# The opening of a two-layer encoder with TensorE in written order up to the first scores

## The chip, the cores and the metric

The kernel runs on one core of a Trainium2 chip. The time is that of one execution on the device, in microseconds. The engines are named as in the profile: PE is TensorE (PEld its weight loads), DVE is VectorE, ACT is ScalarE, POOL is GpSimd, and SP issues most DMAs.

## What is computed

The input is a grid of 512 tokens (8 rows of 64) with 1024 features in float32. There are two residual layers, each followed by a squared-ReLU MLP of width 4096, and a last RMSNorm. Only the first layer's mixing matters here:

```python
hn = rmsnorm(h, norm_mix[0])
z = hn @ w_in                                    # 512 + 128 + 128 + 384 + 256 + 32 columns
qa, ka, va, cq, ckv, kr = jnp.split(z, EVEN_SPLITS, axis=-1)
qa = axial_rope(rmsnorm(qa, a_q_norm), row, col)     # 8 heads of 64
ka = axial_rope(rmsnorm(ka, a_k_norm), row, col)     # 2 heads of 64
oa = block_attention(qa, ka, va, HEAD_DIM ** -0.5)
qb = rmsnorm(cq, b_q_norm) @ b_w_uq              # group B: low-rank query and key/value latents
kvb = rmsnorm(ckv, b_kv_norm) @ b_w_ukv
ob = block_attention(q_full, k_full, vb, (B_NOPE + B_ROPE) ** -0.5)
h = h + concat(oa, ob) @ w_out
```

The second layer is a neighbourhood attention over an 8 x 16 window.

## The kernel before

The activations lie transposed, features on partitions and the 512 tokens along the free axis. Where precision matters an operand is split into two fp32r tiles, a high half (a rounded copy, by ACT) and a low half (the difference, by DVE or POOL), and a product is three matmuls (`mm3`, lines 506 to 508): high by high, high by low, low by high.

**The order of work.** The program is written as one stream. A scheduler arranges each engine's instructions by priority (program order) and by its own estimate of when operands are ready. So before the change TensorE's instructions in the opening do not run as written. Where `tc.manual_schedule` names an engine, that engine follows the program; `tc.keep_in_program_order` does so for one instruction.

**The opening.** Row block k of x (128 features) is transposed by `make_x(k)`, scaled by the norm's gain and split into `X[k]` (lines 545 to 551). `load_w(k)` brings 768 columns of that row block of `w_in`; `use_w(k, m)` adds its three products to bank m. The six banks are the key (m = 0), the value (m = 1) and four pairs of query heads (m = 2 to 5). Row blocks 0 to 5 go bank by bank; then, for each bank, row blocks 6 and 7 close it ("the last rows", lines 759 to 770). `sumsq_acc` adds up the squares of x (line 522); `compact_r` sums them over partitions with the ones vector (line 527) and takes the reciprocal root `r0`, the RMSNorm's scale of each token, which is applied late.

**Behind a bank.** `ev_ka` takes the key: squares by ACT and their sum over each head by a plain fp32 matmul (`stat`, lines 595 and 596), the small transposes that bring the sums to tokens on partitions (`stats_to_tok`, line 580), `rsqrt` on DVE (an integer start and three Newton rounds, lines 159 to 169), the scale spread by transposes (line 535), rotary positions (`rope`, lines 565 to 571), and the split key, whose two halves SP copies across partitions (line 670). `ev_va` transposes the value. `ev_q` does the squares of a query pair (lines 595, 596) and copies the query out (line 608). `q_scales` turns the sums of all eight query heads into scales at once, `rope_q(0)` rotates the first pair (lines 565 to 571) and splits it (lines 622 and 623).

**The attention.** `attend` goes through 64 steps, one for each head and block of 128 queries: scores (line 996), then on DVE scale and row minimum (line 1000, needs the head's scale), ACT's exponential (line 1002), a division by POOL (line 1004), transposes and split of the weights (lines 971 to 974) and the product with the value (line 984). `Fill` puts other TensorE work between these steps, 1.5 us of it for each: first the products for `cq` and `ckv` ("z", columns 768 and up), the latents' norms, then group B's projections. `fill.credit` counts what is owed.

**The end.** `last_mlp` does the last RMSNorm for each of four token blocks: `add` (line 1595), squares with a row sum (line 1599), a root on ScalarE (line 1609), a Newton step on DVE, two scalings and the stores. A placeholder root (line 1656) is written ahead of the second column half.

Of the kernel before, what the change touches and what calls it, by code (L numbers as in the profile page):

```python
# [8 lines left out]
F32 = mybir.dt.float32  # L9
# [26 lines left out]
def encoder_kernel(ctx: ExitStack, tc: tile.TileContext, ins, out, dbg=None):  # L36
# [103 lines left out]
    ACT.activation(act0, zeros, AF.Copy)  # L140
# [383 lines left out]
    def compact_r(acc):  # L524
# [5 lines left out]
        return rsqrt(v, 4)  # L530
# [43 lines left out]
    def stats_to_tok(bk, n, name):  # L574
# [11 lines left out]
        y = rsqrt(v, 4 * n)  # L586
# [4 lines left out]
    QA = []  # L591

    def stat(src, idx, total, lhs, bk, n):
        sq = scratch()
        ACT.activation(sq, src, AF.Square)
        PE.matmul(bk[0:n, :], lhs, sq, start=idx == 0, stop=idx == total - 1)

    def ind1(t):
        return cst[:, C_I1 + 10 * t : C_I1 + 10 * t + 10]
# [4 lines left out]
    QS = [Slot(F32) for _ in range(2)]  # L604

    def ev_q(t, b):
        stat(b, t, 4, ind1(t)[:, 0:8], hold["stq"], 8)
        ACT.activation(QS[t // 2].t[:, S * (t % 2) : S * (t % 2) + S], b, AF.Copy, scale=gT[:, 45:46])

# [41 lines left out]
    def ev_ka(b):  # L651
        st = stb()
        stat(b, 0, 1, ind1(4)[:, 8:10], st, 2)
        kg = scratch()
        ACT.activation(kg, b, AF.Copy, scale=gT[:, 46:47])
        rs = stats_to_tok(st, 2, "rsA")
        krot = rope(kg, cosA, sinA, sw16)
        bk = stb()
        rx = scratch()
        DVE.tensor_copy(rx.rearrange("p (i v e) -> p i v e", i=4, v=2),  # L660
                        rs.unsqueeze(3).to_broadcast([P, 4, 2, 64]))
        bcast_cols(lambda i: rx[:, i * P : (i + 1) * P], P, bk)
        kn = scratch()
        DVE.tensor_tensor(kn, krot, bk, op=ALU.mult)
        for v in range(2):
# [4 lines left out]
            SP.dma_start(f32(kt[z : z + 64, :, :]), f32(kt[a : a + 64, :, :]))  # L670

    def ev_va(b):
        vs = scratch()
        ACT.activation(vs, b, AF.Copy)
        tb = stb()
        for i in range(4):
            PE.transpose(tb[:, i * P : (i + 1) * P], vs[:, i * P : (i + 1) * P], ident)
        for i in range(4):
# [3 lines left out]
                                     op0=ALU.mult, op1=ALU.subtract)  # L682

# [22 lines left out]
    def q_scales():  # L706
        rs = stats_to_tok(hold["stq"], 8, "rsQ")
        sc = keep([P, 4, 8], F32, "scA")
        DVE.tensor_scalar(sc, rs, -0.125, 1.0, op0=ALU.mult, op1=ALU.mult)
        hold["scA"] = sc  # L710
# [46 lines left out]
    sumsq_acc(6, acc)  # L757
    sumsq_acc(7, acc)
    for m in range(6):
        for k in (6, 7):  # L760
            use_w(k, m)
        if m == 0:
            DVE.tensor_copy(r0, compact_r(acc))
            DVE.tensor_tensor(r0sq, r0, r0, op=ALU.mult)
            ev_ka(banks[0])
        elif m == 1:
            ev_va(banks[1])
            hold["stq"] = stb()
        else:
            ev_q(m - 2, banks[m])  # L770
    q_scales()
    rope_q(0)
# [33 lines left out]
    def latents():  # L806
# [4 lines left out]
        sB = stats_to_tok(b, 2, "rsB")  # L811
# [211 lines left out]
    def heads_A():  # L1023
        for h in range(8):
# [13 lines left out]
            yield dict(e=e, done=done, scale=lambda i, h=h: hold["scA"][:, i, h : h + 1],  # L1038
# [50 lines left out]
    fill.add("z", product(w_in, 0, XP, tiles(768, 384), ev_cq, three))  # L1089
# [495 lines left out]
    def last_mlp():  # L1585
# [43 lines left out]
        def down(k0, nk, c, up, tail):  # L1629
# [4 lines left out]
            def run():  # L1634
# [12 lines left out]
                for j in range(4):  # L1647
# [94 lines left out]
```

## Time and profile before

| | us |
|---|---|
| median of 3 runs | 1183.11 (1182.50 to 1183.43) |
| the profiled execution | 1181.52 |
| its span, first to last instruction | 1179.7 |
| its granted TensorE clock | 0.998 of full |

Times within the profile count from the span's start. A row of the order of time gives start, duration, engine, line, operation, what is written and read (by tile name, the buffer's number left out), shapes and a count; in brackets stands how long the engine idled before it and whose signal ended that. A row of the busy time by stage gives a stretch, its length, and the busy microseconds (with the number of instructions) of PE, PEld, DVE, ACT and POOL, then the granted clock, the DMA engines' busy share and GB/s. A row of the grouped instructions gives line, engine, operation, tiles, shape, count, then total busy time and the mean in ns. ACT loads function tables four times in this execution: at 1.78 us, at 3.29 (for line 1656, which the scheduler had moved to the start), at 68.53 (for the exponential of line 1002) and at 1164.28 (for line 1609).

### The profile page before, as it was taken

How to read it: one execution, taken by the hardware profiler on the slowest of the kernel's cores; microseconds unless marked ns; L12 is line 12 of the kernel's file. 1: busy time of each engine (PE TensorE's matmuls, PEld its weight loads, DVE VectorE, ACT ScalarE, POOL GpSimd, SP SyncE). 2: the span in 40 equal slices, each digit the busy share in tenths (PEclk: the TensorE clock that was granted, in tenths of full speed). 3: DMA queues.
4: the chain of work that ended last, by engine and by line, in shares of the span. 5: the costliest groups of instructions: out<-in, count | busy, mean ns of one | idle time of the engine just before them, and what ended most of it. 6: DMA issues, size and time to landing. Idle time of an engine off the chain costs nothing. (4 is left out here: it accounts for less than half of the span.)

```text
span 1179.7 us, 20002 instructions
## 1 busy us (share of the span) xinstructions
PE 1161.2 (98%) x7200; PEld 1019.6 (86%) x7200; DVE 891.2 (76%) x1528; ACT 646.4 (55%) x1097; POOL 540.8 (46%) x683
## 2 busy tenths in 40 slices
PE   9999999999999999999999999999999999999997
PEld 8667788887898999989998998988889899998995
DVE  5588998878866488798884676667986677779775
ACT  5477676764444366743453555555553366664344
POOL 3257242215453878429802232231367458825920
PEclk9999999999999999999999999999999999999999
DMA  7223325222435523225226565433243223342322
GB/s 250 69 58 93 83 57 134 72 63 81 145 88 180 192 73 99 90 90 161 72 73 171 131 174 133 128 106 116 89 153 108 81 73 93 90 133 71 126 73 72
DMA packets 111235, 128.04 MB, mean 109 GB/s; under 512 B 9139, under 2 KB 88928, under 8 KB 111136
## 3 DMA queue, kind: packets, MB, share of 16 engines
q1 hardware_dynamic: 108080, 119.30, 33.7%
q0 software_dynamic: 2304, 6.31, 2.3%
q8 instruction: 57, 0.93, 0.3%
q10 hardware_dynamic: 752, 1.15, 0.3%
q14 instruction: 42, 0.34, 0.1%
HBM read 104.32 MB, written 6.29 MB: 94 GB/s over the span
## 5 line engine op out<-in xcount | busy, mean ns | idle before, releaser
L309 DVE TENSOR_TENSOR wlo<-a,whi 128x896 fp32r<-128x896 f32 x133 | 164.3, 1239 | 76.1 <-ACT whi L308 74.0
L308 ACT ACTIVATE whi<-a 128x896 fp32r<-128x896 f32 x133 | 125.8, 949 | 156.0 <-PE o L507 34.7
L506 PE MATMUL mm<-a,whi 128*128 128x512 f32 x473 | 190.3, 405 | 0.6 <-ACT a L832 0.4
L507 PE MATMUL mm<-a,whi 128*128 128x512 f32 x473 | 187.4, 396 | 0.0
L508 PE MATMUL mm<-a,wlo 128*128 128x512 f32 x473 | 187.0, 396 | 0.0
L202 DVE TENSOR_TENSOR wlo<-raw,whi 128x1024 fp32r<-128x1024 f32 (+4 forms) x113 | 131.6, 1168 | 57.0 <-ACT whi L212 56.7
L302 POOL TENSOR_TENSOR a<-a 128x128 f32<-128x128 f32 x133 | 91.8, 690 | 143.0 <-DMA a<-in_ffn_w_up_dram 96.8
L212 ACT ACTIVATE whi<-raw 128x1024 fp32r<-128x1024 f32 (+3 forms) x116 | 112.0, 967 | 77.4 <-PE s L507 19.4
L303 POOL TENSOR_TENSOR a<-a 128x256 f32<-128x256 f32 x133 | 122.9, 924 | 10.4
L304 POOL TENSOR_TENSOR a<-a 128x128 f32<-128x128 f32 x133 | 112.7, 847 | 10.4
L395 PE MATMUL mm<-a,wlo 128*128 128x256 f32 x390 | 109.8, 282 | 0.7 <-DVE wlo L309 0.7
L393 PE MATMUL mm<-a,whi 128*128 128x256 f32 x390 | 109.6, 281 | 0.0
L394 PE MATMUL mm<-a,whi 128*128 128x256 f32 x390 | 109.4, 281 | 0.0
L508 PEld LDWEIGHTS mm<-a,wlo 128*128 128x128 f32 x473 | 88.6, 188 | 21.6 <-issue 1.7
L506 PEld LDWEIGHTS mm<-a,whi 128*128 128x128 f32 x473 | 88.9, 188 | 20.5 <-issue 1.4
L507 PEld LDWEIGHTS mm<-a,whi 128*128 128x128 f32 x473 | 89.0, 188 | 19.4 <-issue 1.7
L1004 POOL TENSOR_SCALAR p<-p,ti 128x512 f32<-128x512 f32 x64 | 46.3, 724 | 88.3 <-DVE ti L1003 74.3
L1438 POOL TENSOR_SCALAR p<-p,ti 128x256 f32<-128x256 f32 x64 | 35.6, 567 | 105.0 <-DVE ti L1437 91.9
L393 PE MATMUL t<-a,whi 128*128 128x256 f32 x280 | 78.7, 281 | 0.0
L394 PE MATMUL t<-a,whi 128*128 128x256 f32 x280 | 78.6, 281 | 0.0
L395 PE MATMUL t<-a,wlo 128*128 128x256 f32 x280 | 78.5, 280 | 0.0
L395 PEld LDWEIGHTS mm<-a,wlo 128*128 128x128 f32 x390 | 73.4, 188 | 1.5 <-DVE wlo L309 1.5
(335 smaller groups left out, 3251.6 us busy)
## 6 DMA issues: line engine op xcount, KB each, us to landing
a<-in_ffn_w_up_dram SPq DMA_DIRECT2D x100, 256.0 KB
raw<-in_ffn_w_down_dram SPq DMA_DIRECT2D x42, 512.0 KB
a<-in_ffn_w_down_dram SPq DMA_DIRECT2D x33, 256.0 KB
raw<-in_od_w_qkv_dram SPq DMA_DIRECT2D x64, 128.0 KB
raw<-in_ffn_w_up_dram SPq DMA_DIRECT2D x12, 512.0 KB
raw<-in_ev_w_in_dram SPq DMA_DIRECT2D x12, 384.0 KB
a<-a SPq DMA_DIRECT2D x18, 256.0 KB
bias<-bx SPq DMA_DIRECT2D x16, 256.0 KB
```

The costliest lines, as they stand in the source:

```text
L202: z = lambda: (eng or DVE).tensor_tensor(to, src, f32(high), op=ALU.subtract)
L212: ACT.activation(hi[:, 0:m], raw[:, 0:m], AF.Copy)
L303: POOL.tensor_tensor(r[:, 4:6], r[:, 2:3].to_broadcast([P, 2, P]), r[:, 0:7:6], op=ALU.add)
L304: POOL.tensor_tensor(r[:, 7], r[:, 3], r[:, 5], op=ALU.subtract)
L308: ACT.activation(hi[:, 0:896], raw[:, 128:1024], AF.Copy)
L309: DVE.tensor_tensor(lo[:, 0:896], raw[:, 128:1024], f32(hi[:, 0:896]), op=ALU.subtract)
L393: PE.matmul(o, wh, x[:, 0], start=kp == 0 and n in (0, 1, 3, 5), stop=False, skip_group_check=True)
L394: PE.matmul(o, wh, x[:, 1], start=False, stop=False, skip_group_check=True)
L395: PE.matmul(o, wl, x[:, 0], start=False, stop=kp == self.np - 1, skip_group_check=True)
L506: PE.matmul(o, wh, xh, start=first, stop=False)
L507: PE.matmul(o, wh, xl, start=False, stop=False)
L508: PE.matmul(o, wl, xh, start=False, stop=last)
```

## The change

- **TensorE in written order.** From the last rows up to the scales of the last six query heads, TensorE follows the program. `ev_ka` and `ev_va` become generators whose parts are placed between banks by hand. The first z product is made here, and thirteen of its steps (three matmuls each) are placed between the parts; the rest goes to the fill, which starts with a credit of -6.
- **Split squares.** `squares` splits ACT's squares into a high half (DVE copy) and a low half (POOL subtraction) in a slot of its own; `stat` multiplies each half by an fp32r copy of the indicator columns, `ind`.
- **Roots on ScalarE.** `rsqrt_root` takes ACT's Sqrt, DVE's reciprocal and one Newton step. `r0`, the key's scale and the first two heads' scales use it. The first ACT operation is a Sqrt, and an Exp placeholder follows the last root of the opening.
- **The first two heads' scales on their own.** `q_scales` is called for heads 0 and 1 alone, and later for the other six, which keep the Newton start.
- The last two sums of x's squares go from POOL to DVE. The placeholder root of the last stage reads `ss[:, 3:4]`, a result of that stage, in place of a constant.

```diff
-    ACT.activation(act0, zeros, AF.Copy)
+    ACT.activation(act0, zeros, AF.Sqrt)
...
+    def rsqrt_root(v, n):
+
+        root, hv, y, a, y2 = (tiny(n) for _ in range(5))
+        ACT.activation(root, v, AF.Sqrt)
+        DVE.tensor_scalar(hv, v, -0.5, 1.0, op0=ALU.mult, op1=ALU.mult)
+        DVE.reciprocal(y, root)
+        DVE.tensor_tensor(a, y, y, op=ALU.mult)
+        DVE.tensor_tensor(a, a, hv, op=ALU.mult)
+        DVE.scalar_tensor_tensor(y2, a, 1.5, y, op0=ALU.add, op1=ALU.mult)
+        return y2
...
-    def stat(src, idx, total, lhs, bk, n):
-        sq = scratch()
+    ind = keep([P, 50], F32R, "ind")
+    DVE.tensor_copy(ind, cst[:, C_I1 : C_I1 + 50])
+
+    def squares(src):
+
+        sq, t = scratch(), Slot()
         ACT.activation(sq, src, AF.Square)
-        PE.matmul(bk[0:n, :], lhs, sq, start=idx == 0, stop=idx == total - 1)
+        hi, lo = t.pair()[:, 0, :], t.pair()[:, 1, :]
+        DVE.tensor_copy(hi, sq)
+        POOL.tensor_tensor(lo, sq, f32(hi), op=ALU.subtract)
+        return t
+
+    def stat(t, idx, total, lhs, bk, n):
+        for z in range(2):
+            PE.matmul(bk[0:n, :], lhs, t.pair()[:, z, :], start=idx == 0 and z == 0, stop=idx == total - 1 and z == 1)
+        t.free()
...
     def ev_ka(b):
-        st = stb()
-        stat(b, 0, 1, ind1(4)[:, 8:10], st, 2)
+
+        sq = squares(b)
         kg = scratch()
         ACT.activation(kg, b, AF.Copy, scale=gT[:, 46:47])
+        krot = rope(kg, cosA, sinA, sw16)
+        yield
+        st = stb()
+        stat(sq, 0, 1, ind1(4)[:, 8:10], st, 2)
+        yield
         rs = stats_to_tok(st, 2, "rsA")
-        krot = rope(kg, cosA, sinA, sw16)
-        bk = stb()
         rx = scratch()
...
+        yield
+        bk = stb()
         bcast_cols(lambda i: rx[:, i * P : (i + 1) * P], P, bk)
...
-    sumsq_acc(6, acc)
-    sumsq_acc(7, acc)
-    for m in range(6):
+    sumsq_acc(6, acc, DVE)
+    sumsq_acc(7, acc, DVE)
+
+    first_z = product(w_in, 0, XP, tiles(768, 384), ev_cq, three)
+
+    def more(n):
+        for _ in range(n):
+            next(first_z)
+
+    def last_rows(m):
         for k in (6, 7):
             use_w(k, m)
...
+    with tc.manual_schedule(engines={mybir.EngineType.PE}):
+        last_rows(0)
+        ka = ev_ka(banks[0])
+        next(ka)
+        last_rows(1)
+        va = ev_va(banks[1])
+        next(va)
+        DVE.tensor_copy(r0, compact_r(acc, rsqrt_root))
+        DVE.tensor_tensor(r0sq, r0, r0, op=ALU.mult)
+        last_rows(2)
+        ev_q(0, banks[2])
+        next(ka)
+        last_rows(3)
+        next(ka)
+        ev_q(1, banks[3])
+        last_rows(4)
+        rope_q(0)
+        next(va)
+        ev_q(2, banks[4])
+        last_rows(5)
+        next(ka)
+        ev_q(3, banks[5])
+        st0 = stb()
+        stat(hold["sq0"], 0, 1, ind1(0)[:, 0:2], st0, 2)
+        more(3)
+        q_scales(st0, 0, 2)
+
+        tc.keep_in_program_order(ACT.activation(tiny(1), zeros, AF.Exp))
+        more(1)
+        stq = stb()
+        for t in (1, 2, 3):
+            stat(hold[f"sq{t}"], t - 1, 3, ind1(t)[:, 2:8], stq, 6)
+            more(3)
+        q_scales(stq, 2, 6, rsqrt)
...
-    fill.add("z", product(w_in, 0, XP, tiles(768, 384), ev_cq, three))
+    fill.add("z", first_z)
+    fill.credit = -6.0
...
-                        ACT.activation(tiny(1), ones[:, 0:1], AF.Sqrt)
+                        ACT.activation(tiny(1), ss[:, 3:4], AF.Sqrt)
```

More of the change, by code (lines that the diff above doesn't have):

```diff
@@ L522, in sumsq_acc, with compact_r @@
             (eng or POOL).tensor_tensor(acc, acc, sq, op=ALU.add)
-    def compact_r(acc):
+    def compact_r(acc, root=rsqrt):
         b = stb()
@@ L529, in compact_r @@
         DVE.tensor_scalar(v, b[:, 0:4], 1.0 / D, EPS, op0=ALU.mult, op1=ALU.add)
-        return rsqrt(v, 4)
+        return root(v, 4)
     def bcast_cols(col_ap, nparts, bk):
@@ L572, in rope, with stats_to_tok @@
         return c
-    def stats_to_tok(bk, n, name):
+    def stats_to_tok(bk, n, name, root=rsqrt_root):
         st = scratch()
@@ L604, in encoder_kernel @@
     QS = [Slot(F32) for _ in range(2)]
+    scA = {}
     def ev_q(t, b):
-        stat(b, t, 4, ind1(t)[:, 0:8], hold["stq"], 8)
+        hold[f"sq{t}"] = squares(b)
         ACT.activation(QS[t // 2].t[:, S * (t % 2) : S * (t % 2) + S], b, AF.Copy, scale=gT[:, 45:46])
@@ L674, in ev_va @@
         ACT.activation(vs, b, AF.Copy)
+        yield
         tb = stb()
@@ L704, in stat2, with q_scales @@
             POOL.tensor_tensor(sq[:, 0:512], sq[:, 0:512], sq[:, 512:1024], op=ALU.add)
-    def q_scales():
-        rs = stats_to_tok(hold["stq"], 8, "rsQ")
-        sc = keep([P, 4, 8], F32, "scA")
+    def q_scales(bk, h0, n, root=rsqrt_root):
+        rs = stats_to_tok(bk, n, f"rsQ{h0}", root)
+        sc = keep([P, 4, n], F32, f"scA{h0}")
         DVE.tensor_scalar(sc, rs, -0.125, 1.0, op0=ALU.mult, op1=ALU.mult)
-        hold["scA"] = sc
+        for h in range(n):
+            scA[h0 + h] = [sc[:, i, h : h + 1] for i in range(4)]
     mt0 = [512, 640, 0, 128, 256, 384]
@@ L1036, in done @@
                         KA[t // 2].free()
-            yield dict(e=e, done=done, scale=lambda i, h=h: hold["scA"][:, i, h : h + 1],
+            yield dict(e=e, done=done, scale=lambda i, h=h: scA[h][i],
                        passes=lambda i, q=q, k=k, e=e: [(q[:, e, i * P : (i + 1) * P], k[:, z, :]) for z in range(2)],
```

19 lines of the change are left out of this document (5 added, 14 removed).

## The prediction

> **What bounds the kernel now.** I read the page's first line, then the busy time by stage, then the order of time around the stage that the change rewrites.
>
> ```profile
> span 1179.7 us, 20002 instructions
> ```
>
> ```profile
> 48.00:60.00 12.00, 11.97 (x45) 5.89 (x43) 7.14 (x20) 8.18 (x17) 2.57 (x2) 1.00 0.38 99
> 60.00:72.00 12.00, 11.13 (x47) 8.10 (x48) 9.63 (x30) 6.46 (x12) 3.83 (x3) 1.00 0.28 82
> 72.00:84.00 12.00, 10.89 (x67) 8.39 (x65) 9.96 (x29) 10.46 (x24) 6.78 (x10) 1.00 0.20 46
> 84.00:100.00 16.00, 14.58 (x85) 11.95 (x85) 14.37 (x34) 12.66 (x29) 10.77 (x12) 1.00 0.33 91
> ...
> 230.00:1179.00 949.00, 938.38 (x5999) 842.78 (x5997) 710.86 (x1105) 493.50 (x790) 449.93 (x574) 1.00 0.37 110
> ```
>
> The columns are the stretch, its length, then the busy microseconds of PE, PEld, DVE, ACT and POOL, the granted clock and the DMA share. TensorE is busy for 938 of the last 949 us, at full clock (1.00). The change rewrites the opening, and what follows is a queue of TensorE work: a microsecond won or lost on TensorE before about 100 us is carried to the end unless a later wait swallows it. Busy is not full speed, so I price TensorE by the steps from one start to the next:
>
> ```profile
> 57.01 0.40 PE L506 MATMUL mm<-a,whi 128*128 128x512 f32 x1
> ...
> 57.34 1.02 PE L596 MATMUL t<-sc,cst 128*8 128x512 f32 x2
> ...
> 58.29 0.50 PE L507 MATMUL mm<-a,whi 128*128 128x512 f32 x1
> ...
> 58.63 0.40 PE L508 MATMUL mm<-a,wlo 128*128 128x512 f32 x1
> ...
> 60.25 0.39 PE L507 MATMUL mm<-a,whi 128*128 128x512 f32 x1
> ...
> 60.48 0.40 PE L508 MATMUL mm<-a,wlo 128*128 128x512 f32 x1
> ...
> 61.03 0.41 PE L580 MATMUL t<-cst,sc 8*128 8x8 f32 x4
> ...
> 61.37 0.51 PE L507 MATMUL mm<-a,whi 128*128 128x512 f32 x1
> ...
> 65.92 0.50 PE L996 MATMUL s<-a,a 128*128 128x512 f32 x1 [0.55 <-DVE a L623]
> ```
>
> Two dense products start 0.23 apart (60.25, 60.48). One sum of squares (L596, plain fp32) holds TensorE from 57.34 to 58.29, 0.95, and the products on either side of it step by 0.33 and 0.34 instead of 0.23: 1.15 in all. The first scores start at 65.92.
>
> **The change part by part.** *Split squares on TensorE.* Each of the five sums of squares becomes two products with split operands. The dense products above have such operands and step by 0.23, so I price a sum at 0.46 with nothing at its edges: 5 x (1.15 - 0.46) = 3.4 us saved. Scales in two parts cost a second set of small transposes, 0.34 (61.03 to 61.37) and 0.1 at either edge: 0.5 lost. Net 2.9 us.
>
> *Split squares elsewhere* are one DVE copy and one POOL subtraction for each of five tiles:
>
> ```profile
> 35.60:65.90 30.30, 29.32 (x121) 18.39 (x121) 19.61 (x62) 15.02 (x28) 6.38 (x5) 1.00 0.24 62
> ```
>
> ```profile
> 45.93 0.17 DVE L583 TENSOR_TENSOR rsA<-t,r0sq 128x8 f32<-128x8 f32 x1
> ...
> 50.50 0.43 DVE L660 COPY sc<-rsA 128x512 f32<-128x512 f32 x1
> ...
> 64.02 1.30 POOL L202 TENSOR_TENSOR wlo<-raw,whi 128x512 fp32r<-128x512 f32 x1 [4.23 <-ACT whi L212]
> ...
> 64.49 1.37 DVE L623 TENSOR_TENSOR a<-sc,a 64x512 fp32r<-64x512 f32 x1 [0.67 <-ACT a L622]
> ...
> 66.12 0.69 DVE L623 TENSOR_TENSOR a<-sc,a 64x512 fp32r<-64x512 f32 x1
> ```
>
> POOL gets five times 1.3 and loses one sum of that size: 6.4 becomes about 11.5. DVE gets five copies (0.43 each, 2.1) and the last add of x squares (0.69). It loses the integer start and two Newton rounds of two roots, some 14 operations of 0.17 (2.4), and gets about 1.5 for the second scale chain: 19.6 becomes about 21.5, in a stretch that I expect to be 4 us shorter, so DVE goes from 65% to some 82% busy. Beside it stands a collision: L623 began at 64.49 while POOL's L202 ran until 65.32, and took 1.37; its twin, with POOL idle, took 0.69. A subtraction on POOL can so add nothing to a DVE operation, 0.7, or up to its own 1.3. I take 0.7 for two of the five, inside DVE's slack. [...]
>
> *The written order up to the first scores.* I add TensorE's work as the diff writes it, from the start of the last rows:
>
> ```profile
> 35.66 0.50 PE L506 MATMUL mm<-a,whi 128*128 128x512 f32 x1
> ...
> 36.75 0.75 DVE L550 SCALAR_TENSOR_TENSOR a<-t,gT,a 128x512 fp32r<-128x512 f32 x1
> ...
> 38.19 0.63 ACT L520 ACTIVATE sc<-hT 128x512 f32<-128x512 f32 x1 [1.79 <-DVE hT L551]
> ...
> 40.30 1.05 PE L527 MATMUL t<-ones,acc 128*128 128x1 f32 x8 [0.42 <-POOL acc L522]
> ...
> 50.98 0.66 PE L535 MATMUL t<-cst,sc 128*128 128x128 f32 x4
> ...
> 51.40 0.48 PE L506 MATMUL mm<-a,whi 128*128 128x512 f32 x1
> ```
>
> ```profile
> L506 PE MATMUL mm<-a,whi 128*128 128x512 f32 x23 | 9.1, 411 | 0.0
> ...
> L506 PE MATMUL s<-a,whi 128*128 128x512 f32 x4 | 1.7, 422 | 0.0
> ...
> L506 PE MATMUL o<-a,whi 128*128 128x512 f32 x2 | 0.8, 395 | 0.0
> ```
>
> The last rows' 36 products: 8.3. The norm's sum (L527): 1.0. Two blocks of four transposes, for the value and the key's scale, at 0.42 (L535, 50.98 to 51.40): 0.85. Three sets of small transposes: 1.0. Five split sums: 2.3. Thirteen steps of the first z product, of three products each: 9.0. Six visits to plain fp32, 0.2 at the edges of each: 1.2. Together 23.6, which ends at 59.3 if nothing waits. Three waits can't be filled in a fixed order. The first bank's second product of row block 7 needs the low half that L550 ends at 37.50, and is reached at about 36.6: 0.9 (before, products of other banks went ahead). The norm's sum needs the squares (L520, until 38.82) and an add of 0.69, so 39.6, against 39.3 for twelve products and the first wait: 0.3. The key's scale took from 45.93 to 50.93 (L583 to L660) with Newton rounds among DVE's other work; with a root on ScalarE I put it at 2.5 to 5.0, against 3.4 us of TensorE work between its two ends: 0 to 1.6, and I take 0.8, near the low end because two thirds of the Newton work is gone. First scores at 59.3 + 2.0 = 61.3 (60.5 to 64, the late end if the key's last half or a weight tile's low half comes late on a DVE that is 82% busy).
>
> By 65.92 the kernel before has run L506 23 + 4 + 2 = 29 times since 35.6 (the grouped rows above are of that window). Twelve are the last rows, 17 are steps of z; the change has done 13. Four steps are 2.8 us. At equal work the change is ahead by 65.9 - 2.8 - 61.3 = 1.8 us (2.6 to -0.9). This contains the 2.9 us of the sums: the fixed order's waits give back the rest of it.
>
> *Softmax begins at once.*
>
> ```profile
> 68.75 0.75 DVE L1000 CUSTOM_DVE_ANT_0 p<-s,zeros,scA 128x512 f32<-128x512 f32 x1 [0.15 <-DVE scA L709]
> ...
> 95.80 1.10 PE L984 MATMUL o<-a,a 128*128 128x256 f32 x7 [1.11 <-DVE a L974]
> ```
>
> ```profile
> 100.00:110.00 10.00, 10.00 (x60) 8.61 (x59) 6.71 (x15) 7.64 (x18) 7.31 (x10) 1.00 0.28 73
> ```
>
> Softmax now starts at 68.75, 2.8 after the scores, held by the scales of all eight heads. With two heads on their own, their sums reach the small transposes some 8.5 us ahead of the scores (nine steps, three sums, the rest above), at 52.8, and a chain of 2.5 to 5.0 as for the key ends by 57.8. So softmax starts at 62: 6.8 earlier, where TensorE is only 1.8 ahead. From 72 to 100 TensorE idles 1.11 + 1.42 = 2.5 us, waiting for DVE's products of softmax (95.80), with DVE and ACT 80 to 90% busy; from 100 on it is full (10.00). Softmax that is 5 us further ahead takes some of those waits away: between 0 (they are a matter of rate) and 2.5. I take 2.2, because the lead of 5 is twice the sum of the waits.
>
> *Edits with one answer.* The first ScalarE operation as a root merges two table loads at the start, where ScalarE waits for data: nothing. The Exp placeholder moves a load that today stands just before the first softmax: nothing, since it is covered by z products. The fill's debt of 6 us and z's earlier start only shift z among the scores; its weight loads and the key's copies share SP's queue, and a key late by a microsecond is inside the range. At the end, the root's placeholder is to stay in place:
>
> ```profile
> 1164.28 1.28 ACT L1609 ACT_TABLE_LOAD   x1
> ...
> 1170.74 0.40 PE L1642 MATMUL s<-whi,a 128*128 128x512 f32 x1
> ...
> 1171.17 0.69 DVE L1595 TENSOR_TENSOR a<-a,s 128x512 f32<-128x512 f32 x1
> ```
>
> The load of 1.28 us leaves the last stage, but the last add starts at 1171.17, right behind the last product (1171.14), so TensorE sets it: nothing, at most 0.3.
>
> **The sum.** 1.8 + 2.2 = 4.0 us. The profiled execution took 1181.52 us, 1.8 over its span; less 4.0 it is 1177.5. The runs' median lies 1.59 above the profiled execution, so the forecast for a median is 1183.11 - 4.0 = 1179.1.
>
> **The rivals.** *The lead in softmax is worth nothing.* For it: DVE 14.37 of 16 and ACT 10.46 of 12 are rates, not latencies, and DVE gets more work. Against it: TensorE's waits there are single holes, such as the 1.11. Time: 1183.11 - 1.8 = 1181.3.
> *Everything fits.* The key's scale is covered (0.8 more), all 2.5 us of waits go, and so does another 1.0 behind 100: 1183.11 - (1.8 + 0.8 + 2.5 + 1.0) = 1177.0. For it: softmax's lead of 5 us; against it: the 82% DVE.
> *POOL's subtractions hold DVE on the way to the key and the first query.* TensorE's order is fixed, so each microsecond by which the key's scale, the low half of a weight tile or the first key comes late stands on TensorE whole, where before other products went ahead. If each holds a DVE operation for its whole 1.3, DVE needs 21.5 + 6.5 = 28.0 us from 35.6 on. It idled 10.7 of 30.3 before; if 6 of these remain, and the whole list lies ahead of the first query's last half, the scores start at 69.6: 8.3 late, 8.3 - 4.0 = 4.3 slower, 1187.4. It decides from a delay of 6.4, when the gain and the band of no change are used up. For it: the pair of L623; against it: the subtractions come one at a time, with DVE's own gaps between them.
> *The change doesn't do what it says*: the program's order for DVE, ACT and POOL is still chosen by a scheduler, so the key's chain may sit behind other work, with a result between the first rival and no change, 1182.5.
>
> **How the numbers follow.** About 0.2% (2.4 us) is what a measurement of this kernel can tell from no change. Chances: forecast 0.39, everything fits 0.22, softmax lead worth nothing 0.15, order goes astray 0.06, POOL holds DVE 0.18. Faster by over 0.2% (below 1180.7): the forecast (nearly all) and everything fits, 0.60. Within 0.2%: softmax lead worth nothing, order astray, and a hundredth each of the forecast and the POOL case, 0.23. Slower: the rest of the POOL case, 0.17. The range for 8 in 10 goes from 1175.0 (everything fits, with the waits behind 100 gone too) to 1185.5, where the POOL case begins to decide.
>
> **What would show it.** In the profile after: L596 at 0.23 a step; first scores at 61 to 62 with 39 z products done; the first L1000 within 1 us of the scores; TensorE idle from 72 to 100 under 1 us; ACT table loads at the start, before the first softmax and in the gap ahead of the last half, not at L1609. Wrong would be: scores after 64, a DVE operation with two SBUF inputs of 1.3 us or more on the key's chain, or as much idle time between 62 and 100 as before.

## The result and the profile after

The changed kernel took 1188.12 us (median; 1187.11 to 1190.24) against 1182.47 for the kernel before (1181.31 to 1183.43): a ratio of 1.0048 with a 95% interval of 1.0036 to 1.0059. It is 5.6 us slower where 4.0 us faster was forecast, and outside the forecast's range (1175.0 to 1185.5). The profiled execution took 1187.11, with a span of 1185.3. From the page, first line, and from its slices the granted clock in tenths:

```profile
span 1185.3 us, 19993 instructions
...
PEclk9899999999999999999999999999999999999999
```

One slice shows an 8, the second (30 to 59 us); a shorter loss of the clock doesn't show at this width. The busy time by stage of the changed kernel (PE, PEld, DVE, ACT, POOL, granted clock, DMA share, GB/s) narrows it down:

```profile
48.00:60.00 12.00, 7.85 (x26) 5.42 (x27) 11.84 (x20) 7.78 (x15) 5.56 (x4) 0.72 0.23 54
...
72.00:84.00 12.00, 10.97 (x62) 8.53 (x61) 11.16 (x29) 9.56 (x22) 8.16 (x10) 1.00 0.29 82
84.00:100.00 16.00, 16.00 (x94) 13.57 (x94) 11.86 (x29) 12.34 (x27) 11.08 (x12) 1.00 0.23 71
100.00:120.00 20.00, 19.89 (x104) 14.15 (x104) 13.48 (x33) 13.05 (x31) 14.62 (x17) 1.00 0.35 90
...
130.00:140.00 10.00, 6.50 (x33) 5.18 (x34) 8.65 (x22) 3.66 (x7) 1.31 (x1) 0.86 0.56 151
```

The last of these stages in the kernel before:

```profile
130.00:140.00 10.00, 9.72 (x60) 8.15 (x60) 9.52 (x21) 8.24 (x18) 3.91 (x4) 1.00 0.33 92
```

TensorE lost time in two places. From 48 to 60 it was busy for 7.85 of 12 us (11.97 before) while DVE was busy for 11.84 (7.14 before). From 130 to 140 it was busy for 6.50 of 10 (9.72 before). In between it gained: full from 84 to 100 (14.58 before). The order of time on TensorE in the changed kernel shows what it waited for:

```profile
36.95 0.50 PE L518 MATMUL mm<-a,whi 128*128 128x512 f32 x1 [0.60 <-DVE a L561]
...
41.38 0.63 PE L617 MATMUL t<-a,ind 128*2 128x512 f32 x2
41.85 0.39 PE L517 MATMUL s<-a,whi 128*128 128x512 f32 x1
...
48.44 0.63 PE L546 MATMUL t<-cst,sc 128*128 128x128 f32 x4 [1.30 <-DVE sc L686]
...
52.77 1.02 PE L617 MATMUL t<-a,ind 128*2 128x512 f32 x2 [3.71 <-DVE sc L692]
53.58 0.63 PE L517 MATMUL mm<-a,whi 128*128 128x512 f32 x1
54.01 0.63 PE L518 MATMUL mm<-a,whi 128*128 128x512 f32 x1
...
67.18 1.20 PE L1062 MATMUL s<-a,a 128*128 128x512 f32 x4
...
136.59 0.62 PE L546 MATMUL t<-cst,rsB 128*128 128x128 f32 x4 [3.39 <-DVE rsB L598]
```

Two waits for DVE (1.30 and 3.71) stand in the opening and one of 3.39 in the attention, at the scale of group B's latents. From 53.58 to 54.01 a product's step is 0.43 instead of 0.23. Busy time by stage over those two stretches alone gives the granted clock there, 0.50:

```profile
51.82:58.65 6.83, 5.88 (x16) 4.09 (x17) 6.67 (x11) 5.25 (x10) 2.56 (x2) 0.50 0.24 53
137.15:140.56 3.41, 3.41 (x15) 2.52 (x14) 2.63 (x7) 2.49 (x5) 0.00 (x0) 0.50 0.51 114
```

What kept DVE, in the order of time on DVE and POOL (L812 sets the norm's scale, L692 multiplies the rotated key by its spread scale):

```profile
40.60 1.29 POOL L578 TENSOR_TENSOR sc<-sc,a 128x512 f32<-128x512 f32 x1
40.82 1.10 DVE L181 TENSOR_SCALAR ti<-ti 128x4 f32<-128x4 f32 x1
...
42.68 0.69 DVE L582 TENSOR_TENSOR sc<-sc,sc 128x512 f32<-128x512 f32 x1
...
43.85 1.29 POOL L612 TENSOR_TENSOR a<-sc,a 128x512 fp32r<-128x512 f32 x1 [1.97 <-DVE ti L185]
43.88 1.29 DVE L812 COPY r<-ti 128x4 f32<-128x4 f32 x1
...
46.59 0.17 DVE L181 TENSOR_SCALAR ti<-rsA 128x8 f32<-128x8 f32 x1
...
49.33 1.65 POOL L612 TENSOR_TENSOR a<-sc,a 128x512 fp32r<-128x512 f32 x1 [2.81 <-DVE a L611]
...
50.03 1.50 DVE L582 TENSOR_TENSOR sc<-sc,sc 128x512 f32<-128x512 f32 x1
...
52.05 0.67 DVE L692 TENSOR_TENSOR sc<-sc,t 128x512 f32<-128x512 f32 x1
```

A copy of four elements a partition (L812) takes 1.29 us, just as long as the subtraction (L612) that began 0.03 ahead of it; L181 takes 1.10 beside POOL's L578 and, on eight elements a partition, 0.17 without it. Both lie on the way to the key's scale, since its first step (L594, at 45.48) needs the norm's scale. The key's own rotation is done early: the L582 at 42.68 is its last step. The L582 at 50.03 belongs to the first query pair, whose rotation the program writes ahead of L692. The key's scale is spread by 49.07 (L546 above, 48.44 and 0.63), and L692 still waits until 52.05 behind the query's rotation, two steps of the value (L712) and copies of squares (L611). One of these, the L582 at 50.03, takes 1.50 us beside POOL's L612 (49.33 to 50.98), where the one at 42.68 took 0.69: 0.8 us. I added, over all of DVE's instructions from 35 to 67, what each took above the shortest of its operation and shape in the same run: 6.9 us, against 1.5 in the kernel before; I call this DVE's excess. Seven operations, each running beside one of POOL's, make up 6.1 of the 6.9. Over the whole stretch from the last rows to the first scores:

```profile
35.06:67.18 32.12, 26.51 (x115) 18.84 (x114) 25.70 (x56) 17.61 (x34) 12.26 (x9) 0.89 0.20 52
```

The last wait has a different shape. The latents' root is a chain of small DVE operations. In the kernel before they follow each other:

```profile
125.94 0.15 DVE L166 TENSOR_TENSOR ti<-ti 128x8 f32<-128x8 f32 x1
126.12 0.17 DVE L167 TENSOR_TENSOR ti<-ti,ti 128x8 f32<-128x8 f32 x1
126.33 0.58 DVE L169 SCALAR_TENSOR_TENSOR ti<-ti,ti 128x8 f32<-128x8 f32 x1
...
128.14 0.17 DVE L587 TENSOR_TENSOR rsB<-ti,r 128x8 f32<-128x8 f32 x1
```

In the changed kernel one large operation stands between each two of them:

```profile
128.62 0.15 DVE L166 TENSOR_TENSOR ti<-ti 128x8 f32<-128x8 f32 x1
128.70 0.67 DVE L653 TENSOR_TENSOR sc<-sc,sc 128x512 f32<-128x512 f32 x1
129.30 0.15 DVE L167 TENSOR_TENSOR ti<-ti,ti 128x8 f32<-128x8 f32 x1
129.38 0.67 DVE L895 TENSOR_TENSOR a<-mm,a 128x512 fp32r<-128x512 f32 x1
129.98 0.14 DVE L169 SCALAR_TENSOR_TENSOR ti<-ti,ti 128x8 f32<-128x8 f32 x1
...
136.28 0.17 DVE L598 TENSOR_TENSOR rsB<-ti,r 128x8 f32<-128x8 f32 x1
```

From the first `rsB` operation to `scB` there are 14 DVE operations of over 0.4 us in the changed kernel and 4 in the kernel before (one of the chain's own among them each time); the chain takes 11.7 us instead of 5.1.

The remaining signs. The first softmax and the table loads:

```profile
61.48 1.28 ACT L832 ACT_TABLE_LOAD   x1
...
68.30 0.74 DVE L1066 CUSTOM_DVE_ANT_0 p<-s,zeros,scA 128x512 f32<-128x512 f32 x1
...
1166.80 1.28 ACT L1723 ACT_TABLE_LOAD   x1
```

### The profile page after: what moved, and what is told of

It reads as the page before. It is cut to its first block, busy times and chain, and to the rows that moved or that the text cites. A ratio compares the mean times of both kernels' runs of the same rounds, so it can differ in the third digit from the quotient of the medians.

```text
span 1185.3 us, 19993 instructions
## 1 busy us (share of the span) xinstructions
PE 1161.0 (98%) x7204; PEld 1023.8 (86%) x7204; DVE 898.9 (76%) x1531; ACT 646.6 (55%) x1101; POOL 539.6 (46%) x686
## 5 line engine op out<-in xcount | busy, mean ns | idle before, releaser
L313 POOL TENSOR_TENSOR a<-a 128x128 f32<-128x128 f32 x133 | 89.5, 673 | 147.1 <-DMA a<-in_ffn_w_up_dram 114.1
L315 POOL TENSOR_TENSOR a<-a 128x128 f32<-128x128 f32 x133 | 109.7, 825 | 10.4
```

The source lines that it names most:

```text
L315: POOL.tensor_tensor(r[:, 7], r[:, 3], r[:, 5], op=ALU.subtract)
```

## The experiments

**Fourteen kernels.** The first six change one thing in the changed kernel, the next two add one part to the kernel before, and the last six follow the second wait and the parts that were left. Line numbers shift by a few from kernel to kernel. Times are medians; the kernel before, run beside them on the same chip, took 1182.0 to 1182.6.

**e1_bank: another PSUM bank for the first heads' sum.** The wait at L617 might have been one for its bank.

```diff
-        st0 = stb()
+        st0 = sbk()
```

> After, with one edit: the sum for the first two heads goes into a PSUM bank of the pair s instead of the pair t. All engines keep their instructions in the same order. Theory A (a wait for a PSUM bank): both banks of pair t are held, one by the value's transposes until the last L712 (56.5), one by the key's spread scale until L692 (52.7), so the 3.7 us hole before the sum at 52.77 goes; TensorE never idles for over 2 us, its clock stays at 1.0 through the opening, first scores come near 61 in place of 67.2, and the time falls by 4 to 6 us to about 1182.5, the second hole near 133 still costing 3 to 5. Theory B (DVE is late because POOL's subtractions lock it out, and the bank is only where that shows): the hole moves to the next thing that DVE owes, the low half of a z weight tile (L213) or the first query, and the time falls by under 2 us.

1190.65, ratio 1.0067 (1.0052 to 1.0082): 2.5 us slower than the changed kernel, where both expectations had it faster. The sum no longer waits, the wait moved on to the next small transposes and grew:

```profile
57.73 0.59 PE L591 MATMUL t<-cst,sc 2*128 2x2 f32 x4 [5.82 <-ACT sc L588]
```

Now it is L591, the small transposes, that waits: for an ACT copy (L588) which stands in ACT's order behind the value's evacuation and the query's splits, which in turn wait for DVE. So L617 did wait for its bank, which L692 had still to read, but freeing the bank gains nothing: DVE is late all the same.

**e2_warm: nine idle products into the wait.** They feed nothing and only keep TensorE busy, for 2.17 us.

```diff
+        idle_work(9, mmb())
```

> After, with nine useless fp32 matmuls of 128 columns (some 3.6 us) ahead of the sum for the first two heads, so that TensorE works through the hole, and nothing else moved in the written part. Their result goes unused. Theory C (the clock is a cost of its own): the granted clock stays at 1.0 from 52 to 58.6, the twelve products there step by 0.23 and not 0.43, first scores come 2 to 3 us earlier although the hole is as long as before, and the time falls by about 2 to 3 us. Against it: if the half clock only overlaps with waits for DVE, the first scores stay at about 67 and the time within 0.5 us.

1188.54, ratio 1.0052 (1.0035 to 1.0069), as the second expectation had it. The opening kept the full clock (1.00 from 35.93 to 67.67), but the order of time on TensorE shows a new wait behind the first:

```profile
53.85 0.62 PE L617 MATMUL t<-a,ind 128*2 128x512 f32 x2 [1.71 <-DVE sc L692]
...
58.49 0.41 PE L591 MATMUL t<-cst,sc 2*128 2x2 f32 x4 [1.95 <-ACT sc L588]
```

At full clock TensorE runs through its nine z products faster (0.23 a step instead of 0.43) and then waits 1.95 for the copy behind DVE. From the start of the last rows to the first scores it is 31.7 us instead of 32.1. So in the opening the half clock by itself costs some 0.4 us: DVE sets the pace.

**e3_low_dve: the squares' low halves on DVE.**

```diff
-        POOL.tensor_tensor(lo, sq, f32(hi), op=ALU.subtract)
+        DVE.tensor_tensor(lo, sq, f32(hi), op=ALU.subtract)
```

> After, with the low half of the squares made by DVE in place of POOL. Takes five POOL subtractions of 1.3 us (and the blocking that they do to DVE) away and gives DVE five operations of 0.69. Theory B (blocking by POOL makes the key late): the small operations of the root chains take 0.17 each (L181, L812, L596 took 1.10, 1.29 and 0.62), the key's product L692 comes 1 us or more earlier than 52.05, and the time falls by 1 to 4 us. Theory A alone: DVE has 3.4 us more of its own work in the same order, the key comes no earlier, and the time is the same or longer by up to 2 us.

1187.17, ratio 1.0039 (1.0024 to 1.0054): 1 us better, which is within the noise of such a difference. DVE's excess fell from 6.9 to 3.1, but its own work rose by the subtractions, and from 48 to 60 it is busy for 11.39 of 12. TensorE's two waits are still 1.09 and 3.23 us. Where the low half is made hardly matters; DVE is full either way.

**e4_credit: less debt.**

```diff
-    fill.credit = -6.0
+    fill.credit = -1.5
```

> After, with the fill's starting credit at -1.5 in place of -6.0: the rest of z and group B's projections go among the scores three steps sooner. Theory D (the second hole, 3.4 us from 133.2 with a half clock after it, comes from the fill's debt: the latents' norm is reached late and in one burst): the hole shrinks to under 1.5 us, no half clock near 137, and the time falls by 3 to 5 us. Rival: the hole is made by DVE's order at the latents' root and stays as long, only earlier; time within 1 us.

1188.3, ratio 1.0047 (1.0032 to 1.0062). The wait at 133 shrank to 1.31, and another came:

```profile
80.47 0.39 PE L1050 MATMUL o<-a,a 128*128 128x256 f32 x1 [2.11 <-ACT a L1039]
```

The first expectation had the wait right and the time wrong: the time stayed. It looks as if, with z already begun, the credit only chooses which step of the attention lacks cover; one run can't show it.

**e5_plain and e6_free: one half of the opening each.** `e5_plain` keeps the written order and returns to plain fp32 sums; `e6_free` keeps the split squares and leaves TensorE's order to the scheduler.

```diff
# e5_plain
-            PE.matmul(bk[0:n, :], lhs, t.pair()[:, z, :], start=idx == 0 and z == 0, stop=idx == total - 1 and z == 1)
+        PE.matmul(bk[0:n, :], lhs, t.t[:, 0:512], start=idx == 0, stop=idx == total - 1)
# e6_free
-    with tc.manual_schedule(engines={mybir.EngineType.PE}):
+    if True:
```

> After, with the sums of squares plain again: squares stay whole in fp32, one plain fp32 matmul each, no DVE copies, no POOL subtractions; order, roots and scales as in the change. Theory F (DVE is full in the opening, and the split filled it): DVE loses 2.1 us of copies and about 5 us of time blocked by POOL, its excess over the shortest same operation falls from 6.9 to under 2.5 us, the holes ahead of the first scores shrink from 5 to under 2 us in all and the clock stays at 1.0; TensorE pays 3.4 us more for the sums. First scores 2 to 4 us earlier than after, time 2 to 4 us less, about 1185. Rival G (the written order alone is at fault, whatever fills DVE): holes of 4 us or more remain, the half clock too, and the time is 1188 to 1192, since the sums got dearer.

> After, with TensorE's order left to the scheduler in the opening, all else as in the change. Theory F: DVE's list is the same and as full, but while a sum or transpose waits, other products stand ahead of it, so no hole of over 2 us and no half clock before 60; first scores at 63 to 66 with more z products done, time 3 to 5 us below after, 1183 to 1185. Rival G's pure form agrees here; what tells them apart is DVE's excess, which by F stays near 6 us. Against both: the scheduler's order waits as long (first hole over 3 us), time within 1 us of after.

`e5_plain`: 1189.76, ratio 1.0058 (1.0043 to 1.0073). `e6_free`: 1186.88, ratio 1.0035 (1.0022 to 1.0048). If a full DVE were all, they should have been 2 to 5 us under the changed kernel; neither differs from it by more than 1.7. In `e5_plain`, without split squares, DVE's excess is 1.9, the opening keeps full clock (1.00 from 36 to 72) and its two longest waits are 1.49 and 1.21 us, but the sums cost their time again; the other expectation had this time, but with waits of 4 us or more and the half clock. In `e6_free`, with a free order, the first scores come at 63.17, yet DVE's excess is 7.6 and the key's scale is late there too:

```profile
49.64 1.09 PE L546 MATMUL t<-cst,sc 128*128 128x128 f32 x4 [2.73 <-DVE sc L686]
```

Both keep the second wait, of 3.37 and 3.38 us, so neither part makes it.

**e7_split and e8_root: one part on the kernel before.** `e7_split` adds the split squares alone (copy, subtraction, two products for each sum); `e8_root` adds the roots on ScalarE alone, with both placeholders, and uses them for the scales of all eight query heads (the changed kernel keeps the Newton start for six):

```diff
# e8_root
-            DVE.tensor_copy(r0, compact_r(acc))
+            DVE.tensor_copy(r0, compact_r(acc, rsqrt_root))
...
+    tc.keep_in_program_order(ACT.activation(tiny(1), zeros, AF.Exp))
```

> Before, with the split squares alone (DVE copy, POOL subtraction, two fp32r products for each sum), order and roots as before. Price by TensorE's steps: 3.4 us saved, so 1179.1. Theory F: the copies and POOL's blocking take DVE's slack of about 11 us in this stretch without filling it, so most of the saving stays: 1179 to 1181.5. Rival H (POOL's blocking alone makes it a loss, in any order): slower than before by 1 us or more.

> Before, with the roots on ScalarE alone: the norm's, the key's and all eight heads' scales by Sqrt, reciprocal and one Newton step, the Exp placeholder behind them and the tail's placeholder reading ss; order and squares as before. The key's chain shortens by some 2 us and the scales of all heads by as much, so the first softmax operation comes 1 to 2 us earlier than 68.75; TensorE was covered by z products, so the time falls by 0 to 1.5 us: 1181 to 1182.5. Against it: the placeholder holds ScalarE's queue until the last root and the time rises by 1 us or more.

`e7_split`: 1183.06, ratio 1.0006 (0.9996 to 1.0015), no difference, where one expectation had it faster and the other slower by 1 us or more. Its first softmax is at 73.99 instead of 68.75, and TensorE waits 2.38 us for it (until 74.81). `e8_root`: 1179.41, ratio 0.9971 (0.9959 to 0.9982), faster than both kernels and than either expectation. Its scores and softmax:

```profile
61.97 1.10 PE L1008 MATMUL s<-a,a 128*128 128x512 f32 x4
62.79 0.75 DVE L1012 CUSTOM_DVE_ANT_0 p<-s,zeros,scA 128x512 f32<-128x512 f32 x1 [0.15 <-DVE scA L720]
```

The first softmax is 6.0 us earlier than in the kernel before (68.75), with all eight heads' scales together. From 72 to 100 TensorE idles 0.80 us instead of 2.53: these are the waits that the forecast wanted an early softmax to remove.

**e9_debt: the debt alone on e8_root.**

```diff
+    fill.credit = -6.0
```

> The kernel before with the roots on ScalarE, and with the fill's credit set to -6.0 after the opening, as in the changed kernel; nothing else of the change. With the roots alone it took 1179.4. If the debt by itself makes the second wait (3.4 us at 133 in the changed kernel, the latents' scale on VectorE), this kernel shows a TensorE wait of over 2 us between 125 and 140, a half clock behind it, and 1182.5 to 1184.5. If that wait needs the other parts too (z in progress ahead of the fill, two heads' scales apart), no wait of over 1.5 us is there, and the time stays at 1179 to 1181.

1185.64, ratio 1.0032 (1.0022 to 1.0042): 6.2 us over `e8_root`. Neither expectation held: the time is that of the first, but the wait is not at the latents.

```profile
99.27 1.18 PE L1008 MATMUL s<-a,a 128*128 128x512 f32 x4 [2.43 <-DMA a<-sc]
```

TensorE waited for the copies of the next heads' query, with no product of the fill in between (the next one starts at 101.4). Its idle time from 72 to 140 grew by 2.4 us over `e8_root`. At the 44th softmax step, by which both kernels have run as many products of each shape, it is 4.4 us behind (184.11 against 179.71): 2.5 of them are idle time, and 1.9 come from products that follow each other a little more slowly, with a clock of 1.00 in every stage from 36 to 140. What slows them is open.

**e10_lat: the latents ahead of the rotary key.**

```diff
-    fill.add("z", rotary_key())
     fill.add("z", latents())
+    fill.add("z", rotary_key())
```

> The changed kernel with one exchange in the fill: the latents' step stands ahead of the rotary key's, so that the rotary key's 3.7 us of products lie between the latents' sums and the use of their scale. If the second wait is a chain on VectorE that lacks cover on TensorE, the wait at 133 falls from 3.4 to under 1.5 us, the half clock behind it goes, and the time falls by 2.5 to 5 us to 1183.0 to 1185.5. If instead VectorE is simply full there, so that any next step on it is as late, a wait of 2 us or more stands at another line between 125 and 145 and the time stays within 1 us of 1188.

1190.29, ratio 1.0067 (1.0052 to 1.0082): slower than the changed kernel by 2.2, and neither expectation held. Two waits instead of one:

```profile
111.26 1.02 PE L876 MATMUL t<-a,cst 128*2 128x512 f32 x2 [1.40 <-POOL a L736]
...
119.47 0.90 PE L546 MATMUL t<-cst,rsB 128*128 128x128 f32 x3 [2.87 <-DVE rsB L598]
```

The exchange did not give what it was meant to. The latents' step holds its whole chain, the spreading of the scale (L546) included, so the rotary key's products come behind L546 on TensorE (L866, from 124.12). The chain is short here, 5.6 us with 4 large operations, and TensorE still idles, because little of its work lies beside it. That fits a wait which is the chain's length less its cover, but the run can't tell the two expectations' causes apart.

**e11_short: a shorter root for the latents.** It leaves out two of the three Newton rounds, and with them part of the root's accuracy.

```diff
+    def rsqrt_one(v, n):
+        got = []
+        rsqrt_steps(v, n, got.append, 1)
+        return got[0]
...
-        sB = stats_to_tok(b, 2, "rsB", rsqrt)
+        sB = stats_to_tok(b, 2, "rsB", rsqrt_one)
```

> The changed kernel with one Newton round instead of three in the latents' root (part of the root's accuracy is left out): 6 of VectorE's small operations fewer between the latents' sums and their scale. The chain took 9.2 us there, 2.8 in the kernel before. If the chain's length is the cause, each operation dropped takes about 0.7 to 1.0 us with it, the wait of 3.4 us at 133 falls to under 0.5, the half clock goes, and the time falls by 3 to 5 us to 1183 to 1185. If the wait is TensorE running ahead of its data whatever the chain does, it stays over 2 us and the time at 1187 to 1189.

1184.28, ratio 1.0019 (1.0009 to 1.0028): 3.8 us less than the changed kernel.

```profile
133.01 0.62 PE L551 MATMUL t<-cst,rsB 128*128 128x128 f32 x4 [1.10 <-DVE rsB L603]
```

The wait fell by 2.3 us, not to the expected 0.5, and the half clock behind it went (1.00 from 130 to 140). Six of the chain's small operations and what stood between them were worth 3.8 us.

**e12_heads, e13_apart, e14_split: what is left.** `e12_heads` joins `e5_plain` and `e6_free`: plain sums, free order. `e13_apart` takes from it the z products in the opening and the debt; `e14_split` is `e13_apart` with split squares.

```diff
# e13_apart and e14_split
     def more(n):
-        for _ in range(n):
-            next(first_z)
+        pass
...
-    fill.credit = -6.0
+    fill.credit = 0.0
```

> The changed kernel with plain fp32 sums of squares and with TensorE's order in the opening left to the scheduler: the roots, the first two heads' scales on their own, z begun in the opening and the debt remain. With the roots alone the kernel takes 1179.4. If split squares and the written order are what costs, it takes 1177 to 1181, with waits of TensorE before 62 under 1 us each. If the second wait belongs to the fill (z and the debt), it shows again between 125 and 140 with over 2 us, and the time is 1182 to 1185.

> The changed kernel with plain sums of squares, TensorE's order left to the scheduler, no z product taken in the opening ahead of the fill, and no debt: beside the kernel before, the roots on ScalarE and the first two heads' scales on their own are left. With z and debt it took 1185.8, with the roots alone 1179.4. If z in the opening with its debt makes the second wait, no wait of over 1 us stands between 120 and 140, and the time is 1178 to 1181. If the two heads' scales make it, by starting softmax early and filling VectorE behind it, the wait of some 3 us is still there and the time is 1184 to 1187.

> As e13_apart, with the split squares: the whole change but the written order, z in the opening and the debt. Added to the kernel before alone, the split squares made no difference (1.0006). If they save TensorE's time where the scales' chains are short, this kernel is 1 to 3 us under e13_apart. If VectorE's copies and POOL's subtractions take back what TensorE saves, it is within 1 us of e13_apart or up to 2 us over it, with 6 us or more by which VectorE's operations between 35 and 67 exceed their shortest twins.

`e12_heads`: 1185.78, ratio 1.0029 (1.0018 to 1.0041), just over the time of its second expectation and with its wait: there is none of over 0.9 us before 120, and then this:

```profile
133.25 1.09 PE L546 MATMUL t<-cst,rsB 128*128 128x128 f32 x4 [3.37 <-DVE rsB L598]
```

`e13_apart`: 1179.32, ratio 0.9973 (0.9963 to 0.9984). No wait of over 0.9 us anywhere before 250, and the latents' chain is back at 5.1 us with 4 large operations. So z in the opening together with its debt makes the second wait, and costs 6.5 us. By `e11_short` some 3.8 us can be put to that wait and the half clock behind it. At the 44th softmax step, with as many products done but for one transpose, `e12_heads` is 6.2 behind `e13_apart` (186.23 against 180.03): 2.1 of them are idle time, some 1.7 the loss of clock (an estimate from the stage from 130 to 140, which ran at 0.83: 10 x 0.17), and the other 2.4 slower steps (the stages from 36 to 130 ran at 1.00). Its scores and softmax come early:

```profile
58.87 1.20 PE L1055 MATMUL s<-a,a 128*128 128x512 f32 x4
59.64 0.75 DVE L1059 CUSTOM_DVE_ANT_0 p<-s,zeros,scA 128x512 f32<-128x512 f32 x1 [0.42 <-PE s L1055]
```

Softmax starts 3.15 us earlier than in `e8_root`, and the time is the same: as far as this pair shows, the two heads' scales on their own are worth nothing once the roots are short.

`e14_split`: 1181.39, ratio 0.9992 (0.9984 to 1.0001), 2.1 over `e13_apart`, as its second expectation had it at its end. DVE's excess is 7.6, TensorE waits 2.73 us for the key's scale, and one-input operations are held as well (L596 ends at 62.49, POOL's L578 at 62.47):

```profile
59.39 1.94 DVE L213 TENSOR_TENSOR wlo<-raw,whi 128x768 fp32r<-128x768 f32 x1
60.48 1.99 POOL L578 TENSOR_TENSOR sc<-a,a 128x512 f32<-128x512 f32 x1
...
61.25 1.24 DVE L596 TENSOR_SCALAR rsQ<-rsQ 128x8 f32<-128x8 f32 x1
```

**The account.** Each step is the difference of two medians, uncertain by some 1.5 us (the ratios' intervals are about 1.2 us to either side). `e13_apart` also has the key's steps in the program's new order, the last sums of x's squares on DVE and the Newton start for six heads:

| from the kernel before, one part after the other | kernel | us | step |
|---|---|---|---|
| the kernel before | | 1182.5 | |
| roots on ScalarE | e8_root | 1179.4 | -3.1 |
| two heads' scales on their own | e13_apart | 1179.3 | -0.1 |
| z begun in the opening, with its debt | e12_heads | 1185.8 | +6.5 |
| split squares, free order | e6_free | 1186.9 | +1.1 |
| written order | changed kernel | 1188.1 | +1.2 |

The last two depend on each other, and each alone lies within that uncertainty; together they are 2.3. With plain sums the written order costs 4.0 (`e12_heads` to `e5_plain`), and within it the split squares then save 1.6, which is not clear of the noise. The fastest kernels are `e8_root` and `e13_apart`, 3 us under the kernel before.

## Why the prediction was wrong

**The price of a sum held.** Two products of L617 step by 0.47 together (41.38 to 41.85), as forecast with 0.46. The 2.9 us of TensorE's time are there, but at most 1.6 of them reach the end (`e5_plain` to the changed kernel); with a free order the split squares lose time, 1.1 and 2.1.

**The waits of the fixed order failed, and with them the first scores: 61.3 forecast, 67.18 measured.** From the start of the last rows it is 32.1 us instead of 25.6. Forecast were 0.9 for the first low half, 0.3 for the norm's sum and 0.8 for the key's scale. The low half cost 0.8 and the norm's sum nothing. The key's scale and the product behind it cost 1.30 + 3.71 = 5.0: I had taken the scale near its low end and had no term for L692, the product of the rotated key with it. L692 holds the bank of the next sum in TensorE's written order, and on DVE it stands behind the query's rotation. The products at half clock add the rest, but `e2_warm` shows that without them TensorE waits for DVE nearly as long. At equal work (four z steps, 2.8 us) the changed kernel is 67.18 + 2.8 - 65.92 = 4.1 behind at the first scores, where I had 1.8 ahead. Not all of it reaches the end: written order and split squares together are 2.3 in the account.

**DVE's slack was the step behind it.** I had 21.5 us of DVE work at 82%, with 0.7 for two collisions. DVE was busy for 25.70, of which 6.9 is its excess, most of it beside POOL; its own work, 18.8, was under the forecast. The average hid that all of it falls together: 11.84 of 12 from 48 to 60. I had counted collisions only for operations with two SBUF inputs, as in the pair of L623. The rows of L812 and L181 show small one-input operations, in the root's chain, that last until the POOL operation beside them ends: L812 took 1.29 us and ended at 45.17, L612 at 45.14; L181 took 1.10 and ended at 41.92, L578 at 41.89. What holds them the profile does not show.

**The third rival** had the mechanism and, at 1187.4, nearly the time. That is partly chance. It expected scores at 69.6 and no other loss; they came at 67.18, and some 3.8 us (`e11_short`) come from a place that it didn't name. It also put the decision into POOL's subtractions, and `e3_low_dve` shows that DVE's own load does as much. The last rival, that the key's chain may sit behind other work on DVE, names the other half of it: 2.2 of the 3.0 us that L692 comes late are DVE's own work ahead of it.

**What I did not see: the second wait.** "The fill's debt of 6 us and z's earlier start only shift z among the scores" priced these at nothing. They moved the latents by one step of the attention, 21 softmax steps ahead of them instead of 22, and none inside their chain; there evacuations, rotations and low halves of weights alternated with the root's operations on DVE. TensorE idled 3.39 and then ran 3.41 us at half clock. The part is worth +6.5, more than the whole difference, and so weighs more than the opening's waits. That it makes the second wait is shown by `e13_apart` and `e14_split`; what the wait costs, 3.8 of the 6.5, by `e11_short`. Why the scheduler orders DVE so at this step is open, as is what slows TensorE's steps by most of the rest, here and in `e9_debt`. Debt and begun z are not told apart: the debt alone cost 6.2 in `e9_debt` without making this wait, a credit of -1.5 with z begun changed nothing, and no run has z begun without a debt. The two count as one part here.

**Softmax at once** came about in size only. The stages from 72 to 120 idled 1.14 us in all (12 + 16 + 20 less the busy 46.86) against 3.46 before by the same sum (its 100 to 120 was busy for 19.07): 2.3 won, 2.2 forecast. But the first softmax is at 68.30, 0.45 earlier instead of 6.8, so the size is luck, and the 0.8 from 100 to 120 is not due to the lead: `e13_apart`, with softmax at 59.64, was busy for 19.07 there, as the kernel before. Its longer lead gave no time at the end over `e8_root`, as the first rival had it; `e8_root`'s own lead did come with the idle time from 72 to 100 gone.

**The end** cost nothing, as forecast: from TensorE's last product to the end it is 8.61 us, 8.60 before. The table load stands at 1166.80, ahead of the last half, and the one of the opening at 61.48, under z products.

**The root on ScalarE**, which I had only as a part of the key's scale, is the part that pays: 3.1 us alone, with all eight heads' scales on it. I had weighed it in a fixed order, where DVE's other work takes its gain; I take it that in the scheduler's order TensorE has something to do meanwhile, but no run shows that this is the reason.

## What to carry to other kernels

Before writing an engine's order by hand, look at the engine that feeds it slice by slice: if its busy share nears 100% in any stretch (here 11.84 of 12 us) between two hand-set points, each of its delays can become a wait of the ordered engine, where a scheduler that may run other products hides a part of them. Price an edit of a few large operations on POOL by every DVE operation near it, the smallest first, since a small operation in a chain can be held for nearly as long as the POOL operation beside it: here L812 took 1.29 us beside a subtraction of 1.29. Moving filler work is an edit with a price too: follow each dependent chain inside the moved work, here the latents' root, to what will lie beside it at its new place.

## What the runs showed of the hardware

**The clock after a wait.** The kernel before ran at full clock from 4.51 us to its last products (1.00 from 4.51 to 1171); the changed one had 0.50 for 6.83 us around the wait of 3.71 and for 3.41 after that of 3.39. Around the wait of 3.71 the clock fell at 51.82, 2.75 us after the wait began and 0.95 before it ended. A wait of 2.73 (`e6_free`) was followed by a fall too, its stage from 48 to 60 at 0.86; one of 2.43 (`e9_debt`) was not, with 1.00 in both stages around it. Shorter ones were followed by one as well: 2.38 (`e7_split`), with 0.86 from 72 to 84; 2.11 (`e4_credit`), with 0.90 from 72 to 84 and 0.96 from 84 to 100; and 1.80 (`e6_free`), with 0.86 from 60 to 72. So in these runs the length of one wait does not decide. What does decide, no run shows.

**The cost of half clock** was not its length here. In the opening, keeping full clock was worth 0.4 us of 6.83 (31.7 us from the last rows to the first scores in `e2_warm`, 32.1 in the changed kernel), since TensorE then waited for the engine that it had been waiting for before.
